# A gated recurrence block on one core: raw weights as single 2 KB blocks in one ring of six, sums written over them, and one order of products for single and twin pairs

## The chip, the cores and the metric

One core of a Trainium2 chip runs the whole program. The metric is the device time of one execution in microseconds, the median of several runs. A profile is one execution taken by the hardware profiler; its span runs from the first to the last instruction.

## The reference, cut to what matters

One decoder layer on 1024 tokens of width 1024, all in float32:

```
proj = x @ w_in -> q | f | i | og | pool_v | gate_a | gate_b        # w_in: 1024 x 7168
a = HGRN2(q, f, i) -> per-head RMSNorm * sigmoid(og) -> @ w_a       # 8 heads, a recurrence over the tokens
b = per-group linear(causal_mean(pool_v) - pool_v) * pool_scale     # 4 groups, w_pool
mix = (sigmoid(gate_a) * a + sigmoid(gate_b) * b) @ w_out
x = LN(alpha * x + mix)
x = LN(alpha * x + relu(x @ w_up)^2 @ w_down)                       # w_up: 1024 x 4096
```

## The kernel before, in words

**Products.** TensorE (PE) multiplies in a rounded float32 form. To keep accuracy each operand is split in a high and a low part: ScalarE (ACT) writes the rounded copy (L118 for weights, a CAST), VectorE (DVE) the rest (L119), and a product takes three matmuls for each 128 rows of depth: high by high, high by low, low by high (L201, L203, L204 in `prod`). A product of `prod` has a depth of 512, so twelve matmuls, and fills one PSUM bank of 128 x 512.

**Pairs.** Large products are done by Strassen's scheme in Winograd's form: a weight of 1024 rows and 2 x 128 columns is four blocks b11, b12, b21, b22 of 512 x 128 (2 KB in each partition), the tokens four parts a11 to a22 with sums s1 to s4, and seven products take the place of eight. `pair` (L263) holds this for one such pair of column blocks. Its operands are t0 = b11, b21, t3 = b22 - b12, t2 = t3 + b11, t4 = b21 - t2, t1 = b12 - b11 and b22; its products are p1 (t0), p2 (b21), p7 (t3), p6 (t2), p5 (t1), p4 (t4) and p3 (b22). p1, p6, p5 and p3 add up in one PSUM bank, `ps["a"]`; p7 and p4 in `ps["z"]`; p2 has `ps["c"]`. Between them results are taken out: after p1 and p6 ACT copies bank a (L271), after p7 it copies bank z, after p5 DVE adds bank a onto the copy of z (L275). Each of these must end before the next product adds onto that bank.

**Who uses pairs.** In the head stage, one at a time through `run`: `head_inputs` (eight, L643), `output_gates` (four, L674), `pooled` (four, L732) and `gates` (eight, L688). Then `a_pair` (four, L1001) on w_a, two together in `run`, so that their products alternate. Then the up projection on w_up: pairs 0 and 1 together, pair 2 threaded between them (`run_second`, L373), and pairs 3 to 15 singly (L1211). A flag `twin` chooses between two orders: pairs that run together do p1, p2, p7, p4, p6, p5, p3, one operand at a time; single pairs do p1, p2, then t3 and t2 together with p6, p7, then t1 and t4 together with p5, p4, then p3 (L346).

**Raw weights.** Weights come from HBM over the SP queue into raw tiles. `raw_tile` (L206) is a ring of two tiles of 4 KB in each partition; one holds two blocks (b11 and b12, or b21 and b22). Two neighbouring blocks come in one load of 512 KB (L217), two that lie apart in two loads of 256 KB (L223). The sums t are written to a ring of two 2 KB tiles (`w_diff`, L239); t2 and t4 are written over the first of them. So b11 and b12 are free when t1 has been formed, b21 and b22 when b22 has been split. In the up projection every second pair uses a ring of its own (`up_raw_tile`, L1144), and every second w_a pair `mg_raw` (L998). Others borrow `raw_tile` too: the block b22 of the values at the start (L445), rows of w_out (L585), and the weights of the pooled linear (`pool_products`, L708). Split operands go to a ring of ten w tiles of 2 KB (L233), two for each operand.

**What sets the order.** The framework plans the order of every queue ahead of time, with a timing model: at each point an engine gets the earliest instruction of the program that the plan has ready, so that products of the next pair fill in where the pair's own products wait. `high_priority` moves an instruction up; all matmuls of a product but its first have it, so that a product that has begun goes through. The order is then fixed; on the chip each engine's queue, SP's too, runs in that order, and an instruction that waits holds up those behind it. Tiles are given out in the same plan when an earlier one is released.

**The end of the heads.** After the last head's recurrence (`hgrn`, L806; its matmuls L875, L898, L915, L918) the program has gates 4, the pooled linear of group 0, gates 5, group 1, gates 6, groups 2 and 3 and gates 7 (L942). `pool_products` loads pooled rows (L719, by way of L594), splits them in w tiles (L118) and multiplies (L105 to L107). The gates store their sigmoids from L699.

The order of a pair's steps, as it is returned:

```
        return (
            ((t0,), ((t0, p1),)),
            ((b_21,), ((b_21, p2),)),
            *(
                (((t3,), ((t3, p7),)), ((t4,), ((t4, p4),)), ((t2,), ((t2, p6),)), ((t1,), ((t1, p5),)))
                if twin
                else (((t3, t2), ((t2, p6), (t3, p7))), ((t1, t4), ((t1, p5), (t4, p4))))
            ),
            ((b_22,), ((b_22, p3),)),
        )
```

Of the kernel before, what the change touches and what calls it, by code (L numbers as in the profile page):

```python
# [16 lines left out]
P = 128  # L17
# [26 lines left out]
def tile_hybrid_block(  # L44
# [161 lines left out]
    def raw_tile():  # L206
        return wq.tile([P, CH, 2, P], F32, tag="raw", name=nm("raw"), bufs=2)

    def w_blocks(src, c1, c2, tile_of=raw_tile):

        raw = tile_of(), tile_of()

        def load(*which):
            for kh in range(2):
                rows_of = src[kh * HALF : (kh + 1) * HALF, :].rearrange("(k p) c -> p k c", p=P)
                if c2 == c1 + P and len(which) == 2:
                    done = nc.sync.dma_start(  # L217
                        out=raw[kh].rearrange("p k n c -> p k (n c)"), in_=rows_of[:, :, c1 : c1 + 2 * P]
                    )
                else:  # L220
                    for n in which:
                        c = (c1, c2)[n]
                        done = nc.sync.dma_start(out=raw[kh][:, :, n], in_=rows_of[:, :, c : c + P])  # L223
            return done

        return raw, load

    def loaded_blocks(*args):
        raw, load = w_blocks(*args)
        load(0, 1)  # L230
        return raw
# [31 lines left out]
    def pair(raw, rooms, takes, pz_tag="pj", twin=False, pc_tag="pj"):  # L263


        b11, b12, b21, b22 = raw if len(raw) == 4 else (raw[kh][:, :, n] for kh in range(2) for n in range(2))
# [76 lines left out]
        def b_22():  # L343
            return w_part(b22)

        return (  # L346
            ((t0,), ((t0, p1),)),
            ((b_21,), ((b_21, p2),)),
            *(
                (((t3,), ((t3, p7),)), ((t4,), ((t4, p4),)), ((t2,), ((t2, p6),)), ((t1,), ((t1, p5),)))  # L350
                if twin
                else (((t3, t2), ((t2, p6), (t3, p7))), ((t1, t4), ((t1, p5), (t4, p4))))
            ),
            ((b_22,), ((b_22, p3),)),
# [47 lines left out]
    with tc.tile_pool(name="xr", bufs=8, side="right", reuse_waits="tile") as xr:  # L402
# [42 lines left out]
        def raw_tile_rows():  # L445
            return [raw_tile().rearrange("p k n c -> p (k n c)").rearrange("p (k c) -> p k c", c=HALF) for _ in range(2)]
# [171 lines left out]
    with tc.tile_pool(name="tmp", bufs=1, side="right", reuse_waits="tile") as tmp:  # L618
# [89 lines left out]
        def pool_products(g):  # L708
# [6 lines left out]
            raw = raw_tile().rearrange("p k n c -> p (k n c)")[:, : 2 * 2 * P].rearrange("p (k c) -> p k c", c=2 * P)  # L715
# [229 lines left out]
        nxt = head_inputs(0, (None, None, "p6", None, None))  # L945
# [55 lines left out]
        def a_pair(p):  # L1001
            raw = loaded_blocks(w_a, 2 * p * P, (2 * p + 1) * P, raw_tile if p % 2 else mg_raw)
            room = mg_tile("room", 4)
            takes = [gated(2 * p + i, u, p < 2) for u in range(2) for i in range(2)]
            return pair(raw, (c_tile, room, room), takes, "hg", True)
# [76 lines left out]
    with tc.tile_pool(name="wo", bufs=1, side="right", reuse_waits="tile") as mp:  # L1082
        st1 = [None] * 8
        g1, b1 = ln_params(lambda: f(act_tile()).rearrange("p a b -> p (a b)"), ln1_g, ln1_b)
        for k2 in range(0, KT, 2):
            raw = raw_rows(w_out, k2, 1)
            for k in range(2):
                n = len(wo)
                out_row(raw[:, k], (
# [46 lines left out]
    with tc.tile_pool(name="up", bufs=1, side="right", reuse_waits="tile") as up:  # L1136
# [15 lines left out]
        def units(i, raw):  # L1152
# [28 lines left out]
            return pair(raw, (c_tile,) * 3, (take(0), last, take(2), take(3)), "hg", i < 2, "tr" if i == 2 else "pj")  # L1181
# [4 lines left out]
        blocks = [up_blocks(i) for i in range(2)]  # L1186
        for _, load in blocks:
            load(0, 1)
        pairs = [units(i, raw) for i, (raw, _) in enumerate(blocks)]
# [212 lines left out]
```

## Time and profile before

| | |
|---|---|
| median of 3 runs | 1461.98 us (1461.56 to 1463.47) |
| the profiled execution | 1460.19 us, span 1458.5 us |
| mean granted TensorE clock | 0.996 |
| loads of w_in, 256 KB each | 64, median 3.4 us from issue to landing |
| loads of w_up, 512 KB each | 30, median 4.2 us |
| a split of 128 x 512 | 620 ns on ACT (L118), 702 ns on DVE (L119) |
| taking a bank out | 582 ns on ACT (L271), 681 ns on DVE (L275) |

How to read the profile: busy times are the sum of an engine's instructions, in us and as a share of the span; PE is TensorE's matmuls and PEld its weight loads, which overlap them. A matmul's shown time includes its way through the array: matmuls of one stream start every 0.23 us though each is shown with 0.39 us, so a product's time is read from start to start. A row of the timeline has the start, the duration, the engine, the line, the operation and the tiles as out<-in; brackets at its end give the idle time of that engine just before and what ended it. A row of waits has the waiting instruction, what it waited for, and total us, times and the longest. A landing time runs from the issue of a load to its last byte.

### The profile page before, as it was taken

To read this page: it belongs to the slowest core of one execution; us is meant where nothing else is said; L and a number is where in the kernel's file an instruction comes from. 1 tells how busy PE (TensorE), PEld (TensorE's weight loads), DVE (VectorE), ACT (ScalarE), POOL (GpSimd) and SP (SyncE) were. 2 spreads that over 40 slices of the span, in tenths; PEclk is the share of its full clock that TensorE was granted. 3 is DMA by queue.
4 is the path that set the end of the run, shared out by engine and by line. 5 is a ranking of instruction groups with operands and counts; after the bars stand their busy time and mean duration, and the time that the engine had idled before them with its cause. 6 is when DMAs were issued, how large, how long until landed. Compare 5 with 4: busy or idle time off the path is not lost.

```text
span 1458.5 us, 20662 instructions
## 1 busy us (share of the span) xinstructions
PE 1436.4 (98%) x7377; PEld 1187.9 (81%) x7377; DVE 1141.6 (78%) x1838; ACT 758.3 (52%) x1383; POOL 58.6 (4%) x244
## 2 busy tenths in 40 slices
PE   8999999999999998999999999999999999999997
PEld 7888888888888886788888878888888888888886
DVE  5967989899898885768985597666666787777977
ACT  5445565666656655556542376555555443333535
POOL 0001001001000010000002100000000100000000
PEclk9999999999999999999999999999999999999999
DMA  7232233323234447897672225444474874445322
GB/s 253 70 126 87 85 98 101 109 75 114 90 99 138 152 132 249 301 299 241 223 247 99 73 94 195 159 146 144 152 261 149 275 260 150 153 141 163 130 73 116
DMA packets 160615, 226.82 MB, mean 156 GB/s; under 512 B 11232, under 2 KB 84480, under 8 KB 160512
## 3 DMA queue, kind: packets, MB, share of 16 engines
q1 hardware_dynamic: 158576, 218.93, 44.7%
q0 software_dynamic: 1152, 4.19, 0.8%
q10 hardware_dynamic: 784, 2.38, 0.5%
q8 instruction: 58, 0.95, 0.3%
q14 instruction: 45, 0.37, 0.1%
HBM read 154.16 MB, written 71.30 MB: 155 GB/s over the span
## 4 chain that ended last, share of the span: by engine, by line
PE 94%; DVE 3%; DMA 1%; ACT 1%; issue 0%; SPq 0%; DVEq 0%
PE ps_pj L201 16%; PE ps_pj L203 16%; PE ps_pj L204 16%; PE ps_pj L1283 4%; PE ps_pj L1285 4%; PE ps_pj L1284 4%; PE ps_pj L106 3%; PE ps_pj L107 3%; PE ps_pj L105 2%; PE ps_tr L1285 1%; PE ps_tr L1283 1%; PE ps_tr L1284 1%; PE ps_sc L201 1%; PE ps_sc L203 1%; PE ps_sc L204 1%; PE ps_hg L203 1%
## 5 line engine op out<-in xcount | busy, mean ns | idle before, releaser
L201 PE MATMUL ps_pj<-act,w 128*128 128x512 f32 x1068 | 421.6, 395 | 0.4 <-ACT act L123 0.2
L203 PE MATMUL ps_pj<-act,w 128*128 128x512 f32 x1068 | 415.1, 390 | 0.5 <-DVE act L124 0.5
L204 PE MATMUL ps_pj<-act,w 128*128 128x512 f32 x1068 | 414.1, 390 | 0.0
L201 PEld LDWEIGHTS ps_pj<-act,w 128*128 128x128 f32 x1068 | 200.6, 188 | 42.8 <-ACT act L123 0.6
L204 PEld LDWEIGHTS ps_pj<-act,w 128*128 128x128 f32 x1068 | 200.5, 188 | 42.3
L203 PEld LDWEIGHTS ps_pj<-act,w 128*128 128x128 f32 x1068 | 200.6, 188 | 40.6 <-DVE act L124 0.9
L118 ACT CAST w<-t 128x512 fp32r<-128x512 f32 x170 | 104.7, 620 | 105.0 <-PE ps_pj L203 53.8
L118 ACT CAST w<-raw 128x512 fp32r<-128x512 f32 x143 | 88.2, 620 | 117.3 <-PE ps_pj L203 62.5
L119 DVE TENSOR_TENSOR w<-raw,w 128x512 fp32r<-128x512 f32 x143 | 99.8, 702 | 55.2 <-ACT w L118 53.9
L119 DVE TENSOR_TENSOR w<-t,w 128x512 fp32r<-128x512 f32 x170 | 115.9, 685 | 29.6 <-ACT w L118 29.4
L1245 ACT CAST act<-act 128x1024 fp32r<-128x1024 f32 x66 | 66.9, 1050 | 107.9 <-issue 35.0
L1246 DVE TENSOR_TENSOR act<-act,act 128x1024 fp32r<-128x1024 f32 x66 | 79.3, 1220 | 18.5 <-ACT act L1245 15.8
L1285 PE MATMUL ps_pj<-act,act 128*128 128x512 f32 x240 | 92.9, 389 | 0.0
L1284 PE MATMUL ps_pj<-act,act 128*128 128x512 f32 x240 | 92.9, 389 | 0.0
L1283 PE MATMUL ps_pj<-act,act 128*128 128x512 f32 x240 | 92.4, 389 | 0.0
L275 DVE TENSOR_TENSOR c<-c,ps_pj 128x512 f32<-128x512 f32 x95 | 64.5, 681 | 18.0 <-PE ps_pj L204 13.4
L271 ACT COPY c<-ps_pj 128x512 f32<-128x512 f32 x96 | 55.2, 582 | 12.8 <-PE ps_pj L204 12.8
L817 DVE RECIPROCAL tC<-tA 128x128 f32<-128x128 f32 x64 | 54.1, 904 | 0.0
L1284 PEld LDWEIGHTS ps_pj<-act,act 128*128 128x128 f32 x240 | 45.1, 188 | 9.4
L1285 PEld LDWEIGHTS ps_pj<-act,act 128*128 128x128 f32 x240 | 45.1, 188 | 9.4
L1283 PEld LDWEIGHTS ps_pj<-act,act 128*128 128x128 f32 x240 | 45.1, 188 | 9.3
L241 DVE TENSOR_TENSOR t<-raw,raw 128x512 f32<-128x512 f32 x43 | 29.6, 689 | 21.9 <-DMA raw<-in_w_in_dram 19.7
(415 smaller groups left out, 2719.8 us busy)
## 6 DMA issues: line engine op xcount, KB each, us to landing
h<-c SPq DMA_DIRECT2D x106, 256.0 KB, 2.1
act<-h SPq DMA_DIRECT2D x78, 256.0 KB, 2.9
raw<-in_w_in_dram SPq DMA_DIRECT2D x64, 256.0 KB, 3.4
draw<-in_w_down_dram SPq DMA_DIRECT2D x16, 1024.0 KB, 7.8
raw<-in_w_up_dram SPq DMA_DIRECT2D x30, 512.0 KB, 4.2
raw<-in_w_in_dram SPq DMA_DIRECT2D x18, 512.0 KB, 4.0
hf<-h SPq DMA_DIRECT2D x34, 256.0 KB, 2.9
c<-o SPq DMA_DIRECT2D x24, 256.0 KB, 3.4
```

The lines of the kernel that those rows point to most:

```text
L118: A.copy(hi, src)
L119: V.tensor_sub(lo, src, f(hi))
L201: PE.matmul(ps, wh[:, k], th, start=first and k == 0, stop=False, skip_group_check=True)
L203: PE.matmul(ps, wh[:, k], tl, start=False, stop=False, skip_group_check=True)
L204: PE.matmul(ps, wl[:, k], th, start=False, stop=k == CH - 1, skip_group_check=True)
L271: A.copy(t, ps)
L275: V.tensor_add(t, t, ps)
L1245: A.copy(hi, src)
L1246: V.tensor_sub(lo, src, f(hi))
L1283: PE.matmul(ps, hh[:, w], wh, start=fresh and n == 0, stop=False, skip_group_check=True)
L1284: PE.matmul(ps, hh[:, w], wl, start=False, stop=False, skip_group_check=True)
L1285: PE.matmul(ps, hl[:, w], wh, start=False, stop=n == M - 1, skip_group_check=True)
```

## The change

One ring of six 2 KB tiles, `block_tile`, takes the place of both `raw_tile` and the ring of sums. A single pair's four blocks have a tile each and a load of 256 KB each, in the order b11, b21, b12, b22, with a fifth tile for t asked for ahead of b22. In t4 the difference b12 - b11 is written over b12 (t1 then only splits it), t becomes b22 - (b12 - b11), and b21 - t is written over b21. The flag `twin` is gone: every pair has the order that twin pairs had, and the sum of c21 is taken after p6. In the up projection all pairs but pair 1 use the ring (pair 1 keeps up's own tiles); `up_raw_tile`'s second turn for odd pairs is gone, and the loads of w_down start behind the load of b22 of the last pair but one. The wide loads stay for w_a pairs 0 and 2. The values' b22, the rows of w_out and the pool weights use the ring's tiles, the first two with a load for each tile.

```diff
-    def raw_tile():
-        return wq.tile([P, CH, 2, P], F32, tag="raw", name=nm("raw"), bufs=2)
...
+    def block_tile(shape=(CH, P)):
+        return wq.tile([P, *shape], F32, tag="raw", name=nm("raw"), bufs=6)
+
+    def wide_block(src, kh, c, t):
+
+        rows_of = src[kh * HALF : (kh + 1) * HALF, :].rearrange("(k p) c -> p k c", p=P)
+        done = nc.sync.dma_start(out=t, in_=rows_of[:, :, c : c + t.shape[2]])
+        return t, done
...
+    def loaded_blocks(src, c1, c2, done=None):
+
+        raw = {}
+        for i in ((0, 0), (1, 0), (0, 1), "t", (1, 1)):
+            raw[i] = block_tile(), None
+            if i != "t":
+                raw[i] = wide_block(src, i[0], (c1, c2)[i[1]], raw[i][0])
+        if done is not None:
+            done.append(raw[1, 1][1])
+        return [raw[i][0] for i in ((0, 0), (0, 1), (1, 0), (1, 1), "t")]
...
-    def w_diff(a, b):
-        t = wq.tile([P, CH, P], F32, tag="t", name=nm("t"), bufs=2)
-        V.tensor_sub(t, a, b)
-        return t
...
         def t3():
-            c["t"] = w_diff(b22, b12)
+            c["t"] = block_tile() if t is None else t
+            V.tensor_sub(c["t"], b22, b12)
             return w_part(c["t"])
 
-        def t2():
-            if not twin:
-                V.tensor_add(c["t"], c["t"], b11)
-            return w_part(c["t"])
-
         def t4():
-            if not twin:
-                V.tensor_sub(c["t"], b21, c["t"])
-                return w_part(c["t"])
-            V.tensor_add(c["t"], c["t"], b11)
+            V.tensor_sub(b12, b12, b11)
+            V.tensor_sub(c["t"], b22, b12)
             V.tensor_sub(b21, b21, c["t"])
             return w_part(b21)
 
+        def t2():
+            return w_part(c["t"])
+
         def t1():
-            return w_part(w_diff(b12, b11))
+            return w_part(b12)
...
                 c[21] = copied(rooms[1], ps["a"])
-                if twin:
-                    takes[2](added(c[21], ps["z"]))
+                takes[2](added(c[21], ps["z"]))
 
         def p4(w):
             prod(ps["z"], w, "a22", False)
-            if not twin:
-                with tc.high_priority(PRIO):
-                    takes[2](added(c[21], ps["z"]))
...
+        return tuple(
+            ((operand,), ((operand, product),))
+            for operand, product in ((t0, p1), (b_21, p2), (t3, p7), (t4, p4), (t2, p6), (t1, p5), (b_22, p3))
         )
...
-        raw = raw_tile().rearrange("p k n c -> p (k n c)").rearrange("p (k c) -> p k c", c=HALF)
-        rows_of = src[k2 * P : (k2 + 2) * P, cc * HALF : (cc + 1) * HALF].rearrange("(k p) c -> p k c", p=P)
-        nc.sync.dma_start(out=raw, in_=rows_of)
+        raw = [block_tile((HALF,)) for _ in range(2)]
+        for k in range(2):
+            nc.sync.dma_start(out=raw[k], in_=src[(k2 + k) * P : (k2 + k + 1) * P, cc * HALF : (cc + 1) * HALF])
         return raw
...
-            raw = raw_tile().rearrange("p k n c -> p (k n c)")[:, : 2 * 2 * P].rearrange("p (k c) -> p k c", c=2 * P)
+            raw = block_tile((2, 2 * P))
...
-        def up_blocks(i):
-            return w_blocks(w_up, i * 2 * P, i * 2 * P + P, up_raw_tile if i % 2 else raw_tile)
...
         for i in range(3, NP):
-            raw, load = up_blocks(i)
-            w_load = load(0, 1)
+            done = []
+            raw = loaded_blocks(w_up, i * 2 * P, i * 2 * P + P, done)
             if i == NP - 2:
                 for part in down_rows(0, ws0):
-                    part(w_load)
+                    part(done[0])
             run(units(i, raw))
```

More of the change, by code (lines that the diff above doesn't have):

```diff
@@ L204, in prod, with wide_blocks @@
                 PE.matmul(ps, wl[:, k], th, start=False, stop=k == CH - 1, skip_group_check=True)
-    def raw_tile():
-        return wq.tile([P, CH, 2, P], F32, tag="raw", name=nm("raw"), bufs=2)
[L209 to L231, printed above, removed]
+    def block_tile(shape=(CH, P)):
[4 more added lines that the diff above has]
+        return t, done
+    def wide_blocks(src, c1, tile_of):
+        raw = [wide_block(src, kh, c1, tile_of().rearrange("p k n c -> p k (n c)"))[0] for kh in range(2)]
+        return [raw[kh][:, :, n * P : (n + 1) * P] for kh in range(2) for n in range(2)]
+    def loaded_blocks(src, c1, c2, done=None):
[7 more added lines that the diff above has]
+        return [raw[i][0] for i in ((0, 0), (0, 1), (1, 0), (1, 1), "t")]
     def w_tile():
@@ L261, in c_late, with pair @@
         return c_tile(False)
-    def pair(raw, rooms, takes, pz_tag="pj", twin=False, pc_tag="pj"):
-        b11, b12, b21, b22 = raw if len(raw) == 4 else (raw[kh][:, :, n] for kh in range(2) for n in range(2))
+    def pair(raw, rooms, takes, pz_tag="pj", pc_tag="pj"):
+        b11, b12, b21, b22, t = raw if len(raw) == 5 else (*raw, None)
         c, ps = {}, {}
@@ L445, in raw_tile_rows @@
         def raw_tile_rows():
-            return [raw_tile().rearrange("p k n c -> p (k n c)").rearrange("p (k c) -> p k c", c=HALF) for _ in range(2)]
+            return [block_tile((1, HALF)) for _ in range(4)]
         def load_block(tiles, kh, nh, ks=None):
@@ L1001, in a_pair @@
         def a_pair(p):
-            raw = loaded_blocks(w_a, 2 * p * P, (2 * p + 1) * P, raw_tile if p % 2 else mg_raw)
+            cols = 2 * p * P, (2 * p + 1) * P
+            raw = loaded_blocks(w_a, *cols) if p % 2 else wide_blocks(w_a, cols[0], mg_raw)
             room = mg_tile("room", 4)
             takes = [gated(2 * p + i, u, p < 2) for u in range(2) for i in range(2)]
-            return pair(raw, (c_tile, room, room), takes, "hg", True)
+            return pair(raw, (c_tile, room, room), takes, "hg")
         def unpark(*which):
@@ L1088, in tile_hybrid_block @@
                 n = len(wo)
-                out_row(raw[:, k], (
+                out_row(raw[k], (
                     (lambda: (row_tile(), row_tile())) if n < 10 else
@@ L1179, in last @@
                 put(6, s4)
-            return pair(raw, (c_tile,) * 3, (take(0), last, take(2), take(3)), "hg", i < 2, "tr" if i == 2 else "pj")
-        def up_blocks(i):
-            return w_blocks(w_up, i * 2 * P, i * 2 * P + P, up_raw_tile if i % 2 else raw_tile)
[L1186 to L1189, printed above, removed]
+            return pair(raw, (c_tile,) * 3, (take(0), last, take(2), take(3)), "hg", "tr" if i == 2 else "pj")
+        blocks = loaded_blocks(w_up, 0, P), wide_blocks(w_up, 2 * P, up_raw_tile)
+        pairs = [units(i, raw) for i, raw in enumerate(blocks)]
         run(pairs[0][1:2])
```

11 lines of the change are left out of this document (1 added, 10 removed).

## The prediction

> **What bounds the kernel now.** I read the page first: the engines' shares, then the chain that ended last.
>
> ```profile
> span 1458.5 us, 20662 instructions
> PE 1436.4 (98%) x7377; PEld 1187.9 (81%) x7377; DVE 1141.6 (78%) x1838; ACT 758.3 (52%) x1383; POOL 58.6 (4%) x244
> PE 94%; DVE 3%; DMA 1%; ACT 1%; issue 0%; SPq 0%; DVEq 0%
> ```
>
> PE is busy for 1436.4 of 1458.5 us and carries 94% of the chain. The change alters no matmul, so all that it can win is 22.1 us of idle PE. The view of stages says where that idle time lies (columns: stretch, its length, busy us of each engine, granted clock, DMA share, GB/s).
>
> ```profile
> 0.00:30.00 30.00, 26.09 (x137) 22.18 (x137) 13.89 (x29) 16.71 (x31) 2.07 (x28) 1.00 0.79 281
> 30.00:574.90 544.90, 543.86 (x3400) 451.05 (x3400) 469.71 (x889) 315.45 (x680) 37.29 (x202) 1.00 0.35 112
> 574.90:592.00 17.10, 10.35 (x42) 7.54 (x41) 9.22 (x16) 7.69 (x21) 0.00 (x0) 0.80 0.77 255
> 592.00:858.00 266.00, 265.85 (x1203) 219.62 (x1201) 202.32 (x330) 123.56 (x215) 14.78 (x6) 1.00 0.61 205
> 858.00:870.00 12.00, 10.80 (x45) 8.02 (x44) 12.00 (x22) 7.82 (x15) 0.00 (x0) 1.00 0.30 89
> 870.00:1136.00 266.00, 266.00 (x1175) 220.29 (x1174) 178.12 (x271) 157.17 (x266) 0.00 (x0) 1.00 0.50 171
> 1450.00:1458.50 8.50, 0.00 (x0) 0.00 (x0) 5.34 (x9) 0.29 (x1) 0.00 (x0) 0.63 0.32 123
> ```
>
> The first 30 us (3.9 us idle, waiting for x and starting up) and the last norm (8.5 us) are out of the change's reach. The heads (30 to 574.9) lose 1.0 us, the up projection (870 to 1136) nothing. One place is worth something: 574.9 to 592, where PE idles 17.10 - 10.35 = 6.75 us; 858 to 870 adds 1.20 us. The view of PE's waits names them:
>
> ```profile
> PE ps_pj L105 <- ACT w L118: 4.7, 1, 4.7
> PE ps_hg L915 <- DVE st L883: 1.2, 1, 1.2
> PE ps_pj L106 <- DVE w L119: 0.8, 1, 0.8
> ```
>
> At 577 us the last head's recurrence is still running and the next matmul in PE's queue is the pooled product of group 0 (L105). The timeline shows why that one is late, and what else could have run:
>
> ```profile
> 559.09 0.93 SPq L223 DMA_DIRECT2D raw<-in_w_in_dram  x2
> 561.72 1.89 SPq L223 DMA_DIRECT2D raw<-in_w_in_dram  x2
> 564.90 0.34 SPq L594 DMA_DIRECT2D v<-po  x1
> 573.10 0.34 SPq L699 DMA_DIRECT2D gb<-c  x1
> ```
> ```profile
> 582.18 0.62 ACT L118 CAST w<-og 128x512 fp32r<-128x512 f32 x1 [2.75 <-DMA og<-po]
> 582.85 0.79 PE L105 MATMUL ps_pj<-w,q 128*128 128x512 f32 x1 [4.66 <-ACT w L118]
> ```
> ```profile
> 587.41 1.13 ACT L118 CAST w<-raw 128x512 fp32r<-128x512 f32 x2
> ```
> ```profile
> raw<-in_w_in_dram SPq DMA_DIRECT2D x4, 256.0 KB, 5.9
> ```
>
> SP stands still from 564.90 to 573.10 on a store (gb<-c), so the pooled rows (og<-po) come late. gates(5), whose products need nothing from that head, got its four blocks at 559.09 and 561.72, each landing about 5.9 us later, as it waited for the two 4 KB tiles that gates(4) and the pool weights of group 0 held. Its first casts stand at 587.41, behind the pooled rows. PE ran out of other products.
>
> **The change part by part.** One product is twelve matmuls:
>
> ```profile
> 899.76 0.39 PE L201 MATMUL ps_sc<-act,w 128*128 128x512 f32 x1
> 902.25 0.39 PE L204 MATMUL ps_sc<-act,w 128*128 128x512 f32 x1
> 902.48 0.39 PE L201 MATMUL ps_pj<-act,w 128*128 128x512 f32 x1
> 902.98 0.58 ACT L271 COPY c<-ps_sc 128x512 f32<-128x512 f32 x1
> 910.41 0.39 PE L204 MATMUL ps_sc<-act,w 128*128 128x512 f32 x1
> 910.64 0.39 PE L201 MATMUL ps_pj<-act,w 128*128 128x512 f32 x1
> 910.89 0.69 DVE L275 TENSOR_TENSOR c<-c,ps_sc 128x512 f32<-128x512 f32 x1 [1.65 <-PE ps_sc L204]
> ```
>
> 902.48 - 899.76 = 2.72 us a product, 19.0 us a pair.
>
> *Sums in place.* A single pair had four sums on DVE (L241 twice, L284, L289) and has four after it (one in t3, three in t4), of the same shape; the seven splits stay. Nothing gained or lost in DVE work. They are bunched: the operand of p4 now has three sums in a row ahead of its split, 3 x 0.69 = 2.1 us. Operands are made up to five ahead (ten w tiles, two each), so 2.1 us against 4 x 2.72 = 10.9 us of products costs nothing; without that lead it would cost up to 1.4 us a pair.
>
> *The ring.* Six tiles of 2 KB replace two of 4 KB and two of 2 KB: 12 KB before and after. A pair takes five (four blocks and the sum). The sixth lets the next pair's b11 load a whole pair ahead; b21 follows when b11 of the pair before is read for the last time (t4), b12 after the split of t4, b22 after that of t1. Before, the next pair's four blocks waited for t1 and for the split of b22, the very last operand. So in the heads the blocks come earlier by up to three operands, about 8 us. There PE doesn't wait for them, so that wins nothing, except before 592: gates(5) has b11 and b21 some 8 us earlier, about 551 instead of 559 to 562, landed by 557. Then p1 and p2 of gates(5), 2 x 2.72 = 5.4 us, can be put ahead of the pooled products. Bounds: nothing (the planner keeps the pooled rows first) and all 6.75 us. I take 5.4, the two products whose blocks come early; what is late next is the rest of the 6.75, the recurrence's own L915.
>
> *The up projection* had two tile pairs in turn (raw and up's own), a whole pair of lead; now the ring alone. b22 of the next pair is asked for after t1, two products' operands from the end, and is needed three operands into the next pair: about 5 x 2.72 - 2 = 11 us against a landing of 3.4 us (256 KB row below), so it is covered. If SP's queue held it for 8 us, as at 564.90, each pair could lose a few us. The w_down loads are now issued behind the fourth block of the last pair but one:
>
> ```profile
> 1075.66 1.99 SPq L1132 DMA_DIRECT2D draw<-in_w_down_dram  x4
> ```
> ```profile
> 1136.40 0.39 PE L1283 MATMUL ps_pj<-act,act 128*128 128x512 f32 x1
> ```
>
> That is later by about a pair, 19 us, at 1095; 4 MB at the 255 to 281 GB/s of the two busiest stages above is 15 to 16 us more, so they are there at 1111, some 25 us ahead of first use. Nothing.
>
> *More and smaller loads.*
>
> ```profile
> raw<-in_w_in_dram SPq DMA_DIRECT2D x64, 256.0 KB, 3.4
> raw<-in_w_up_dram SPq DMA_DIRECT2D x30, 512.0 KB, 4.2
> raw<-in_w_in_dram SPq DMA_DIRECT2D x18, 512.0 KB, 4.0
> ```
>
> 18 loads of w_in become 36 and 30 of w_up become 58; w_a and w_out add 8: 54 issues more, at 0.3 to 0.5 us each on a queue that is mostly waiting. Two halves of 3.4 us overlap each other, so a full 512 KB lands later than 4.2 us and no later than 6.8; the first half sooner. Hidden by PE's backlog; uncovered it is 2.6 us a pair. The Trainium skill speaks against this part: "DMA: Bandwidth & Descriptors", Bandwidth, tells authors to batch loads to 1 MiB or more. By that rule alone the sum would move toward that 2.6 us for each pair; the rows agree that the bytes cost more in halves, and say that PE isn't waiting for them.
>
> At the start b22 of the values takes four tiles, so two are free and head 0's first two blocks load some 45 us early. Their operands would take four of ten w tiles in a stage that uses eight. Bounds: -1.0 us (the idle time of that stage filled) to about +3 (a split of 0.62 + 0.69 us late at two steps); I take 0.
>
> *The order of products.* p6, p7, p5, p4, p3 becomes p7, p4, p6, p5, p3. The data dependences are the same: p6, p5 and p3 add onto one bank and each waits for the evacuation of the last, as p4 does for p7's copy. Before, another product of the pair stood between each. Now p6, p5, p3 are neighbours and PE needs a foreign product in between. The copy ended 902.98 + 0.58 - 902.25 = 1.31 us after the product's last matmul began, the add 1.17 us after; laid bare, less the 0.23 us until the next matmul's slot, each is about 1.0 us. The order is planned by readiness: p6 can go ahead of p4, p4 between p6 and p5, and p1 or p2 of the next pair between p5 and p3. One such product covers 2.72 us. In the heads DVE is 469.71/544.90 = 86% busy and the add after p5 comes later:
>
> ```profile
> 201.22 0.39 PE L204 MATMUL ps_pj<-act,w 128*128 128x512 f32 x1
> ```
> ```profile
> 203.91 0.67 DVE L275 TENSOR_TENSOR f<-f,ps_pj 128x512 f32<-128x512 f32 x1
> ```
>
> Here it ended 3.36 us after the last matmul began, 3.13 us after its slot: 0.4 us more than one product covers; two cover it. Bounds: 0, and 38 single pairs x 3 x 1.0 = 114 us. I take 1.0 us in all, near the lower end, because the row of the heads shows PE full with the same dependences.
>
> The Trainium skill, "Perfetto Trace Analysis", Matmuls, says that independent matmul groups should rotate through PSUM banks so that one's evacuation overlaps the next. The new order of a single pair goes against it; the old one agreed, with its idle-free stages. By the rule the sum is the rival "bare evacuations" below.
>
> **Sum.** The profiled execution took 1460.19 us (span 1458.5). -5.4 + 1.0 = -4.4 gives 1455.8. The median of the runs, 1461.98, lies 1.8 above it, so the forecast is **1457.6 us**.
>
> **Rivals.** (1) *The gap stays.* The pooled products hold their place ahead of gates(5), because SP's stall and the recurrence set that order and not the weights. For it: og<-po is what ended ACT's wait at 582.18. Then -0 + 1.0: 1463.0, between 1460 and 1464.5.
>
> (2) *Bare evacuations: slower.* If in the heads only one foreign product is ready between p5 and p3, each of the 24 pairs there pays 0.4 us, 10 us, and the gap stays: 1472. It decides from the point where p2 of the next pair has no operand when p5 ends. Against it: earlier blocks make operands earlier. For it: four pj banks, which two running pairs fill. If nothing is ready at even one of the three places, 38 x 1.0 = 38 us: 1500.
>
> (3) *Late blocks.* SP's queue holds b21 or b22 in the up projection; 12 pairs x 1 us, gap closed: 1469. Against it: the 11 us above.
>
> (4) *It doesn't do what it says*: the planner keeps the old product order wherever readiness decides; then only the ring counts, 1456.6, inside the forecast.
>
> **How the numbers follow.** Forecast with (4) 0.47, gap stays 0.23, bare evacuations 0.24 (of it 0.04 for the large form), late blocks 0.06. The forecast's own range is 1454 (all 6.75 and the 1.2 us won: 1461.98 - 7.95) to 1459. The range over the cases is 1454 to 1474: it holds (1), the small form of (2) and (3), and leaves the large form out. Two kernels can be told apart from about 0.2%, 2.9 us: below 1459.1 is faster, 0.47; up to 1464.9 the same, 0.23; slower 0.30.
>
> **What would show it.** In the changed profile: between 575 and 592 PE's idle time falls from 6.75 to about 1 to 2 us and L118 casts of gates(5) stand ahead of those of the pooled rows; from 30 to 575 and from 870 to 1136 PE's busy time stays within 1 us of the stretch; no wait of L201 on L271 or L275 exceeds 1 us in total; loads of w_up land around 3.4 us. Bare evacuations would show as waits of L201 for L271 or L275, tens of times; late blocks as waits of L118 for raw that pass on to PE. I am wrong if PE's idle time grows in the heads or in the up projection, or if a gap opens elsewhere because the new order moves other work.

## The result and the profile after

The changed kernel takes **1467.94 us** (median of 9 runs, 1464.55 to 1471.46), the kernel before 1462.68 us beside it (9 runs). The ratio is **1.0032** (95% interval 1.0019 to 1.0045): slower by 4.7 us where 4.4 us of gain were forecast. The nine runs spread over 7 us and the granted clock of a run goes with them: 0.999 in the fastest, 0.993 in the slowest. The profiled execution took 1467.26 us, its span is 1465.5 us.

The head of the page, and the view of stages (stretch, its length, busy us of each engine with the number of its instructions, granted clock, DMA share, GB/s):

```profile
span 1465.5 us, 20835 instructions
PE 1441.2 (98%) x7377; PEld 1189.9 (81%) x7377; DVE 1137.4 (78%) x1838; ACT 756.8 (52%) x1383; POOL 56.2 (4%) x244
```
```profile
0.00:30.00 30.00, 25.60 (x127) 22.12 (x128) 13.09 (x28) 17.31 (x31) 2.06 (x28) 1.00 0.86 298
30.00:574.90 544.90, 540.17 (x3375) 446.60 (x3374) 468.68 (x888) 312.03 (x677) 35.34 (x202) 1.00 0.35 111
574.90:592.00 17.10, 17.10 (x83) 14.42 (x82) 9.21 (x18) 8.71 (x21) 0.00 (x0) 0.93 0.64 207
592.00:858.00 266.00, 261.66 (x1170) 214.57 (x1169) 195.43 (x323) 119.71 (x211) 14.39 (x6) 0.99 0.62 207
858.00:870.00 12.00, 11.29 (x52) 8.47 (x51) 11.71 (x21) 7.45 (x14) 0.00 (x0) 1.00 0.18 56
870.00:1136.00 266.00, 265.14 (x1170) 219.13 (x1169) 175.83 (x270) 154.78 (x263) 0.00 (x0) 1.00 0.50 167
```

Read the matmul counts, not only the busy time: both kernels have the same 7377 matmuls, so the number begun by a given time says how far each has come, and it also sees matmuls that run slowly, which count as busy. The gap at 574.9 to 592 is gone: 83 matmuls and no idle time, where 42 had 6.75 us of it. But the kernel got there late: 10 matmuls fewer in the first 30 us, 25 fewer from 30 to 574.9. By 592 it is only 3 ahead (3581 against 3578, counted in one stretch from 0; the rows count a matmul that lies across a border twice). From 592 to 858 it begins 33 fewer than before (1170 against 1203), with 4.34 us idle against 0.15. By 870 it is 23 behind (4799 against 4822), at 0.23 us each 5.3 of the 7.0 us by which the two profiled spans differ: most of the loss is made before the up projection starts. From 870 to 1136 it loses 5 more.

The view of PE's waits (waiting instruction, what for, us in total, times, longest) names new entries that the kernel before doesn't have:

```profile
PE ps_pj L201 <- ACT c L264: 3.2, 2, 2.1
PE ps_pj L105 <- ACT q L118: 3.0, 1, 3.0
PE ps_pj L457 <- ACT act L123: 2.0, 1, 2.0
PE ps_hg L204 <- DVE w L119: 0.9, 1, 0.9
```

The third stands at the start. The timeline of ACT there, of before and then of after:

```profile
7.56 0.58 ACT L123 CAST act<-ps_tr 128x512 fp32r<-128x512 f32 x1
10.59 0.62 ACT L118 CAST w<-b 128x512 fp32r<-128x512 f32 x1 [2.45 <-DMA b<-in_w_in_dram]
```
```profile
7.51 0.62 ACT L118 CAST w<-b 128x512 fp32r<-128x512 f32 x1 [2.48 <-DMA b<-in_w_in_dram]
10.55 1.14 ACT L118 CAST w<-b 128x512 fp32r<-128x512 f32 x2 [2.42 <-DMA b<-in_w_in_dram]
11.71 1.05 ACT L123 CAST act<-ps_tr 128x512 fp32r<-128x512 f32 x2
```

Before, ACT made the first activation part (L123) at 7.56 and then waited for the third row of the values' weights. After, the casts of the third and fourth row stand ahead of it in ACT's queue, so it comes at 11.71. PE, whose first real product needs it, pauses (before, then after):

```profile
10.13 0.48 PE L477 MATMUL ps_pj<-w,act 128*128 128x512 f32 x1
```
```profile
12.32 0.50 PE L457 MATMUL ps_pj<-w,act 128*128 128x512 f32 x1 [2.01 <-ACT act L123]
```

The edit didn't touch this code's order. The plan drew a new order around the new ring.

### The profile page after: what moved, and what is told of

Its sections match the earlier page's. It is cut to its first block, busy times and chain, and to the rows that moved or that the text cites. A ratio compares the mean times of both kernels' runs of the same rounds, so it can differ in the third digit from the quotient of the medians.

```text
span 1465.5 us, 20835 instructions
## 1 busy us (share of the span) xinstructions
PE 1441.2 (98%) x7377; PEld 1189.9 (81%) x7377; DVE 1137.4 (78%) x1838; ACT 756.8 (52%) x1383; POOL 56.2 (4%) x244
## 4 chain that ended last, share of the span: by engine, by line
PE 85%; DMA 7%; DVE 5%; issue 1%; ACT 1%; SPq 1%; DVEq 0%; ACTq 0%
PE ps_pj L201 15%; PE ps_pj L203 15%; PE ps_pj L204 15%; PE ps_pj L1260 4%; PE ps_pj L1261 4%; PE ps_pj L1259 4%; DMA raw<-in_w_in_dram 2%; PE ps_pj L105 2%; PE ps_pj L107 2%; PE ps_pj L106 2%; PE ps_tr L1261 1%; PE ps_tr L1260 1%; PE ps_tr L1259 1%; PE ps_hg L204 1%; DMA draw<-in_w_down_dram 1%
## 5 line engine op out<-in xcount | busy, mean ns | idle before, releaser
L201 PE MATMUL ps_pj<-act,w 128*128 128x512 f32 x1068 | 422.9, 397 | 5.2 <-ACT c L264 3.2
L204 PE MATMUL ps_pj<-act,w 128*128 128x512 f32 x1068 | 414.3, 391 | 0.0
L118 ACT CAST w<-raw 128x512 fp32r<-128x512 f32 x311 | 191.7, 622 | 251.1 <-PE ps_pj L203 157.6
L119 DVE TENSOR_TENSOR w<-raw,w 128x512 fp32r<-128x512 f32 x311 | 211.6, 686 | 79.6 <-ACT w L118 76.7
L201 PEld LDWEIGHTS ps_pj<-act,w 128*128 128x128 f32 x1068 | 200.9, 188 | 50.4 <-ACT c L264 3.8
L204 PEld LDWEIGHTS ps_pj<-act,w 128*128 128x128 f32 x1068 | 200.8, 188 | 42.4
L264 ACT COPY c<-ps_pj 128x512 f32<-128x512 f32 x96 | 55.7, 582 | 11.7 <-PE ps_pj L204 6.2
L273 DVE TENSOR_TENSOR raw<-raw,raw 128x512 f32<-128x512 f32 x43 | 29.6, 689 | 26.0 <-DMA raw<-in_w_in_dram 22.5
L1130 ACT ACTIVATE c<-c 128x512 f32<-128x512 f32 x61 | 38.7, 634 | 1.5
L1129 ACT ACTIVATE c<-c 128x512 f32<-128x512 f32 x46 | 29.1, 633 | 15.5 <-DVE c L268 15.5
```

Of the source, the lines that this page charges most:

```text
L118: A.copy(hi, src)
L119: V.tensor_sub(lo, src, f(hi))
L201: PE.matmul(ps, wh[:, k], th, start=first and k == 0, stop=False, skip_group_check=True)
L204: PE.matmul(ps, wl[:, k], th, start=False, stop=k == CH - 1, skip_group_check=True)
L264: A.copy(t, ps)
```

## The experiments

All ratios are to the kernel before on the same chip, with a 95% interval; 0.001 is 1.5 us. "The ring" stands for the ring of six with the sums in place, "the order" for single pairs in the twin pairs' sequence.

**1. The two parts alone.** My first theory (A) was that the ring wins and the order loses.

```diff
 # ring alone: after, with the flag and the old sequence of single pairs back
+    def pair(raw, rooms, takes, pz_tag="pj", twin=False, pc_tag="pj"):
 # order alone: before, every pair as a twin
-    def pair(raw, rooms, takes, pz_tag="pj", twin=False, pc_tag="pj"):
+    def pair(raw, rooms, takes, pz_tag="pj", twin=True, pc_tag="pj"):
```

> The ring of six with the sums in place, but single pairs in their old order (t3 and t2 with p6, p7, then t1 and t4 with p5, p4). Theory A (the ring wins, the order loses): the idle time of PE at 575 to 592 is closed by 5.4 us as in the changed kernel, the waits of L201 on copies of a bank (3.2 us in the changed kernel) are gone, and the time is 4 to 6 us below before, 1457 to 1459. Rival B (any change re-plans all queues, and the kernel before had a lucky plan): PE's idle time falls in one place and opens in another, and the time lies within 3 us of before or above it. Rival C (the ring is what costs): it is slower than before by 4 us or more.

> The kernel before, with its two rings, and every single pair in the twin pairs' order of operands and products. Theory A: the gap at 575 to 592 stays (some 6 us of idle PE) and bare evacuations come on top, 3 to 6 us: 1466 to 1469. Rival B: within 3 us of the changed kernel either way, with gaps at places that neither had. Rival C: as fast as before, 1461 to 1464.

Measured: the ring alone 1.0054 (1.0042 to 1.0066), the order alone 1.0008 (1.0000 to 1.0017). It is the other way round, and theory A falls: the part that I gave a gain costs most, the part that I feared costs 1.2 us. The two don't add up: together they stand at 1.0032, so with the ring in place the order takes 3.2 us off, and neither figure is a price that holds in the other kernel. The ring alone has the start's wait too (2.0 us), the order alone doesn't.

**2. Two other orders of the changed kernel.** The third group's pooled products ahead of gates 6, and p6 ahead of p4 in single pairs of the heads.

```diff
-("gates", 6), ("pool_products", 2), ("pool_products", 3), ("gates", 7),
+("pool_products", 2), ("gates", 6), ("pool_products", 3), ("gates", 7),
```
```diff
+            steps[3:5] = [((t4, t2), ((t2, p6), (t4, p4)))]
```

> The changed kernel, with the pooled linear of group 2 put ahead of gates 6, so that group 3's weights don't ask for a room that group 2's store has only just left. If the new gap at 642 to 645 us (3.0 us of idle PE, and matmuls at a lower clock behind it, 5.5 us in that stretch of 50 us) comes from that wait of ACT on the store, it goes and the time falls by 3 to 5 us below the changed kernel, to 1463 to 1465. If another wait stands behind it, the time stays within 1.5 us of the changed kernel's 1467.9.

> The changed kernel, with p6 ahead of p4 in single pairs (operands t4 and t2 made together, then p6, then p4, and the sum of c21 after p4), so that a product of the pair itself stands between p7 and p4 and between p6 and p5. Theory A (bare evacuations cost 3 to 5 us): the waits of L201 on a bank's copy fall from 3.2 us to under 1 us, and the time falls by 2 to 4 us to 1464 to 1466. Rival B: those waits go or stay, but the time is set by other gaps of the new plan and lies anywhere from 1460 to 1472.

Measured: 1.0085 (1.0070 to 1.0099) and 1.0064 (1.0052 to 1.0076). Both are slower than the changed kernel. With p6 ahead of p4 PE waits for casts instead (2.9 us, L201 on L118) and for the recurrence; with pooled products put earlier three evacuations are bare (4.8 us, L201 on L264). Neither order is a cure.

**3. Is it the recurrence?** The last step of the last head's recurrence on DVE (before, then after):

```profile
589.58 0.74 DVE L932 SCALAR_TENSOR_TENSOR og<-ps_tr,prm,og 128x512 f32<-128x512 f32 x1
```
```profile
598.22 0.75 DVE L912 SCALAR_TENSOR_TENSOR og<-ps_tr,prm,og 128x512 f32<-128x512 f32 x1
```

It ends 8.6 us later. Theory B: earlier blocks let the pairs' operand work go ahead of the recurrence on DVE (86% busy in the heads), and PE lacks work in the end. Four runs: the recurrence put first in the plan of after and, as control, of before; a ring of five with a tile of its own for t; and the start's order taken back.

```diff
-                with tc.high_priority(PRIO_LAST) if (h, u) == (HEADS - 1, 1) else nullcontext():
+                with tc.high_priority(PRIO_LAST if (h, u) == (HEADS - 1, 1) else 300):
```
```diff
 # ring of five
-        return wq.tile([P, *shape], F32, tag="raw", name=nm("raw"), bufs=6)
+        return wq.tile([P, *shape], F32, tag="raw", name=nm("raw"), bufs=5)
...
-            c["t"] = block_tile() if t is None else t
+            c["t"] = wq.tile([P, CH, P], F32, tag="t", name=nm("t"), bufs=1) if t is None else t
```
```diff
 # start as before
-        w = parts(b11)
+        w = parts(b11[:2])
+        with tc.issue_after(made_hi["a11", "first"]):
+            w += parts(b11[2:])
```

The last one comes close to the old order and isn't quite it: all four first casts of the activations stand ahead of the third row now, where before only one did.

> The changed kernel with one edit: the instructions of the heads' recurrence take precedence in the order that the plan writes out, so that fewer of VectorE's instructions for the pairs stand ahead of each half's last step (550 ahead of the seventh head's second half where the changed kernel has 560, 358 ahead of the fourth head's first where it has 375). Theory B (the ring lets the pairs' operand work go ahead of the recurrence on VectorE, the recurrence ends later, and TensorE lacks work at the end of the heads): the last half ends near 590 us where it ended at 598, and the time falls by 3 to 6 us, to 1462 to 1465. Rival R (the loss is made of unrelated places where the plan put the queues in another order: the start's 2 us, the pool weights' 3 us, the 2 us of evacuations): within 1.5 us of the changed kernel, 1466.5 to 1469.5, even though the recurrence ends earlier. A third way, that products then lack operands in the heads because their work stands behind the recurrence: idle time of TensorE from 30 to 550 us grows by over 3 us.

> The kernel before with the same single edit as the run above, as its control: the recurrence takes precedence in the plan. Theory B: there the recurrence was hardly held up, since the pairs' blocks came late (562 instructions ahead of the seventh head's first half's successor, 562 with the edit too), so the time stays within 2 us of the kernel before, 1460 to 1464; what the edit wins in the changed kernel it doesn't win here. Rival R: any new order of the plan costs some us wherever it falls: 1465 or more. If it wins 3 us or more here too, then the recurrence was late before as well, and the edit tells nothing about the ring.

> The changed kernel with a ring of five 2 KB tiles and one 2 KB tile by itself for the sums, so that the sixth tile no longer carries the next pair's first block a whole pair ahead. Theory B: less lead, so the recurrence is held up less in the fifth to seventh heads' first halves (371 and 402 instructions ahead where the changed kernel has 375 and 417), though hardly less at the last half (562 for 560 and 570 for 583): 1463 to 1466. Rival R: no relation to the lead: 1466.5 to 1470, or worse where the blocks now come late.

> The changed kernel with only the start's order on ScalarE as it was before: the third and fourth casts of the values' rows of blocks stand behind the first casts of the activations, not ahead of them. Both theories take the wait of TensorE at 10.3 to 12.3 us (2.0 us for an act tile) for a cost of that order: the wait goes, and the time falls by 1.5 to 2.5 us, to 1465.5 to 1466.5. If the time stays within 0.7 us, the 2 us are given back later, where TensorE waits for the heads' recurrence and not for its own backlog of products.

Measured: recurrence first 1.0019 (1.0010 to 1.0028), its control 0.9992 (0.9983 to 1.0001), ring of five 1.0013 (1.0000 to 1.0026), **start as before 1.0002 (0.9992 to 1.0012)**. With the recurrence first it did end earlier, at 592.21:

```profile
592.21 0.74 DVE L912 SCALAR_TENSOR_TENSOR og<-ps_tr,prm,og 128x512 f32<-128x512 f32 x1
```

6 us earlier bought about 1.9 us, less than B asked. The start's order, which I put at 1.5 to 2.5 us, took back 4.4, and the kernel stands level with the one before. PE begins early again, and its stages follow:

```profile
10.18 0.48 PE L458 MATMUL ps_pj<-w,act 128*128 128x512 f32 x1
```

```profile
0.00:592.00 592.00, 585.18 (x3596) 485.49 (x3597) 494.08 (x937) 338.84 (x733) 37.97 (x230) 1.00 0.39 125
592.00:870.00 278.00, 273.49 (x1227) 223.04 (x1225) 208.91 (x345) 130.28 (x229) 14.38 (x6) 1.00 0.59 198
```

against these of the kernel before:

```profile
0.00:592.00 592.00, 580.30 (x3578) 480.77 (x3578) 492.82 (x933) 339.85 (x732) 39.36 (x230) 0.99 0.38 125
592.00:870.00 278.00, 276.65 (x1246) 227.65 (x1245) 214.32 (x350) 131.38 (x229) 14.78 (x6) 1.00 0.59 200
```

By 592 it is 18 matmuls ahead, 4.1 us: the filled gap. By 870 it is one behind: 4.51 us idle from 592 to 870, where it was 1.35. What the gap gave is given back there.

**4. The start alone, and the gains together.** The start's new order put into the kernel before; the start taken back in the ring alone; and together with the ring of five and with the recurrence first.

```diff
 # before, with the start's order of after
+            with tc.issue_after(last_hi[0]) if name == "a11" and not kp else nullcontext():
+                in_parts(name, kp, ps)
```

(`last_hi[0]` is the cast of the values' fourth row.)

> The kernel before with one edit: ScalarE's order at the start is that of the changed kernel (the casts of the third and fourth row of the values' first block stand ahead of the first cast of the activations); the rest of VectorE's order in the heads is the same count for count. Theory S (the start's order alone makes most of the loss): TensorE waits some 2 us for an act tile at about 10 us and the time rises by 2 to 4.4 us (4.4 is what taking this order back won in the changed kernel: ratios 1.0032 and 1.0002): 1465.5 to 1468 against 1463.5 for the kernel before. Rival: in the kernel before the 2 us are given back in the 9 us at 575 to 600 us where TensorE waits for the recurrence, and the time rises by less than 1 us.

> The ring alone (single pairs in their old order) with the start's order as it was before. The ring alone stood at a ratio of 1.0054. If the start's order is the ring's only price, taking it back leaves nothing: ratio 0.999 to 1.002. If the ring also holds up the recurrence (theory B: with the ring alone the halves of the sixth to eighth head ended 5 to 18 us later than before, and TensorE idled 22 us from 500 to 700 where it idles 13 before), then 1.002 to 1.005 stay: 1466.5 to 1471.

> The changed kernel with the start's order as before and the ring of five with a tile of its own for the sums. If the two gains add (4.4 us for the start and 2.7 us for the ring of five, from the ratios 1.0032, 1.0002 and 1.0013): ratio 0.9983, 1461, faster than the kernel before. If the second is only the order in which the same idle time is spent at the end of the heads, it doesn't come on top: ratio 0.9995 to 1.001.

> The changed kernel with the start's order as before and precedence for the recurrence. If the gains add (4.4 us and 1.9 us): ratio 0.9989, 1462. If the precedence only moves idle time between 575 to 600 us and 600 to 700 us: ratio 0.9998 to 1.001. TensorE's idle time from 500 to 700 us should stay between 13 and 17 us either way, as in all orders so far but those with the ring alone and with the pooled products put earlier.

Measured: the start in the kernel before 1.0022 (1.0012 to 1.0031), so that order alone costs 3.2 us in a kernel that has nothing else of the change. The ring alone falls from 1.0054 to 1.0011 (0.9997 to 1.0024); ring of five from 1.0013 to 0.9997 (0.9988 to 1.0006); recurrence first from 1.0019 to 1.0018 (1.0009 to 1.0027). With the changed kernel (4.4 us) and the pair of experiment 5 (1.0044 to 1.0033) that makes six pairs that differ by this edit alone: 4.4, 6.3, 2.3, 0.1, 1.6 and 3.2 us, **3.0 on the mean**.

The traces show the price more directly. Read instruction by instruction, the queues of PE, ACT and DVE differ within a pair up to 92 us at most; behind that, three pairs (those of the changed kernel, of the kernel before and of experiment 5) have the same order to the end, and the others differ in a few instructions from 575 us on. So the first 100 us hold this price and little else. The changed kernel, then the one with the start as before:

```profile
0.00:100.00 100.00, 94.82 (x444) 78.63 (x445) 71.93 (x123) 48.49 (x84) 2.79 (x34) 1.00 0.47 159
```
```profile
0.00:100.00 100.00, 96.65 (x456) 80.64 (x457) 72.10 (x123) 50.11 (x87) 2.78 (x34) 1.00 0.49 164
```

That is 12 matmuls, 2.8 us; in the other five pairs it is 14 to 19, 3.2 to 4.4 us, always the same way. It is more than the wait of 1.9 to 2.0 us partly because of the granted clock: in six of the eight profiled kernels with this order it falls behind the wait, in none of the ten without. The first 30 us of the kernel before with this order (0.94, where the kernel before has 1.00):

```profile
0.00:30.00 30.00, 24.73 (x120) 20.93 (x121) 11.81 (x25) 16.43 (x30) 2.06 (x28) 0.94 0.79 281
```

The rest of the scatter arises late, and not only from other orders: in the pair of the changed kernel, with the same queues behind 75 us, PE's wait for the fourth group's pool weights near 640 us is 3.0 us in one and 1.1 in the other.

Theory B falls as the main cause: with the start cured, recurrence first is slower than without (1.0018 against 1.0002).

**5. The gap, filled as predicted.** I had said that earlier blocks would put p1 and p2 of gates(5) ahead of the pooled products. The rows of after (SP, then ACT, then PE):

```profile
546.37 0.38 SPq L212 DMA_DIRECT2D raw<-in_w_in_dram  x1
...
547.58 0.38 SPq L212 DMA_DIRECT2D raw<-in_w_in_dram  x1
```
```profile
586.27 0.62 ACT L118 CAST w<-v 128x512 fp32r<-128x512 f32 x1 [0.17 <-DMA v<-po]
586.80 1.66 ACT L118 CAST w<-raw 128x512 fp32r<-128x512 f32 x3
```
```profile
591.18 0.39 PE L201 MATMUL ps_pj<-act,w 128*128 128x512 f32 x1
```

The blocks are asked for 13 us earlier than before (546.4 against 559.1), more than predicted, and then lie for some 37 us: their first cast still stands behind the pooled rows' and p1 of gates(5) starts at 591.18, before it was 589.50. What filled the gap were products of gates(4), whose operands had been cast by 563 us. So theory Q: the order, not the weights, keeps gates(5) out. One edit puts it ahead, in four kernels:

```diff
-("pool_products", 0), ("gates", 5), ("pool_products", 1),
+("gates", 5), ("pool_products", 0), ("pool_products", 1),
```

> The changed kernel with one edit: gates(5) stands ahead of the first group's pooled products in the program, so that the plan puts p1, p2 and p7 of gates(5) ahead of them in TensorE's queue. Theory Q (the queue's order, not the weights, kept gates(5) out of the gap): its first product starts near 570 instead of 591, the idle time from 500 to 700 us falls from 16.5 to about 11, and the time falls by 4 to 6 us, from a ratio of 1.0032 to about 0.9995 (1462 to 1463.5). Rival: idle time there is bound by the recurrence and the pooled rows behind it, whatever fills it; it moves and stays at 13 to 17 us: ratio 1.0025 to 1.004.

> The same edit, with the start's order as before too. Theory Q: both gains add, ratio 0.996 to 0.998, 1457 to 1460, which is where the prediction had the change. Rival: nothing on top of the start's gain, ratio 0.9995 to 1.001.

> The kernel before, without the ring, with gates(5) ahead of the first pooled products. Its blocks are asked for at 559 to 562 and land about 6 us later, 565 to 568, so p1 and p2 could start at about 569 all the same. If the order alone decides: the gap fills here as well, ratio 0.996 to 0.998, and the ring isn't needed for it. If the earlier blocks are needed as well: p1 comes later, the gap stays at more than half, ratio 0.9985 to 1.001.

> Ring of five with a tile of its own for the sums, the start as before, and gates(5) ahead of the first pooled products. It stood at 0.9997 without the last edit. Theory Q: 0.996 to 0.998. Rival: 0.9990 to 1.0005.

Measured: in the changed kernel 1.0044 (1.0030 to 1.0058), with the start as before 1.0033 (1.0022 to 1.0043), in the kernel before 1.0033 (1.0022 to 1.0045), with ring of five and start 0.9991 (0.9982 to 0.9999). In the first of them p1 of gates(5) starts near 570, as theory Q wanted, 21 us earlier than in the changed kernel:

```profile
570.43 0.39 PE L201 MATMUL ps_pj<-act,w 128*128 128x512 f32 x1
```

The time gets worse all the same, and PE's idle time from 500 to 700 us hardly moves: 7.9 us against 8.1 in the changed kernel (the 16.5 of the expectation isn't what the view shows there). That is the rival's outcome. The stages of the second and the third kernel:

```profile
0.00:592.00 592.00, 584.67 (x3591) 484.93 (x3591) 492.10 (x932) 338.05 (x731) 37.96 (x230) 1.00 0.38 122
592.00:870.00 278.00, 272.37 (x1213) 222.26 (x1214) 210.29 (x343) 128.44 (x226) 14.40 (x6) 0.99 0.60 203
```
```profile
0.00:592.00 592.00, 581.77 (x3590) 483.22 (x3591) 493.32 (x935) 337.69 (x721) 39.43 (x230) 1.00 0.38 123
592.00:870.00 278.00, 269.55 (x1200) 219.16 (x1200) 204.84 (x331) 128.42 (x230) 14.75 (x6) 0.99 0.59 201
```

Both are 12 to 13 matmuls ahead of the kernel before at 592, and 33 and 46 behind it from there to 870. Getting ahead by 592 is no gain by itself, with the ring or without it (where 4.0 of the gap's 6.75 us stay idle). That the work used as filling is then missing behind the gap is my reading; no run shows it apart from the waits that each new order brings. Theory Q is right about the order and wrong about the time. Of these four only the last comes out below the kernel before, 1462.16 us against 1462.87, 0.7 us in the medians and 1.3 by the ratio. It is hardly more than level, and the kernel before with the recurrence first (0.9992) is as fast without the ring.

## Why the prediction was wrong

- **What bounds the kernel** was right: PE, with one gap worth naming. What failed is that I took that gap's idle time for reachable time. The changed kernel has none of it and is slower. Two readings beside it were wrong. I put the first 30 us out of the change's reach: they lost 10 matmuls. And idle time isn't all that can be won or lost: busy time grew by 4.8 us with the same matmuls, since slow ones count as busy (the last section).
- **The ring, -5.4 us: this step failed.** Its first half held and went further than predicted (blocks 13 us earlier, not 8). The second half, that p1 and p2 of gates(5) are put ahead of the pooled products, didn't happen: ACT's queue kept them behind. That was half of the rival "the gap stays": the pooled rows held their place, but the gap was filled by other products. And where an edit did put them ahead, the gain was given back between 592 and 870.
- **The start, taken as 0: mis-sized.** It measured 3.0 us over six pairs, the upper end of my bound (-1 to +3), by another mechanism: I looked at spare w tiles and late splits, and what cost was ACT's order at 10 us. It comes with the ring (both rings have it, the order alone doesn't). With it taken back the change measures 1.0002. So 5.4 us of gain that didn't come and 3.0 us of cost make 8.4 of the 9.1 us between forecast and result (9.8 with the 4.4 us of the changed kernel's own pair); what remains is within the scatter. That 1467.94 lies in the range of 1454 to 1474 is luck: the range reached so far up for bare evacuations and late blocks, and the start's order was in none of the cases. The sign of being wrong that I named did come, PE's idle time in the heads (30 to 574.9) grew from 1.0 to 4.7 us.
- **The order of products, 1.0 us**: 1.2 us alone, the size that I had, but the interval reaches down to nothing and with the ring the sign was the other (experiment 1). In the changed kernel two evacuations were bare for 3.2 us, beyond the 1 us that I had allowed. The longer one shows how, in ACT's timeline and PE's:

```profile
562.25 0.62 ACT L118 CAST w<-raw 128x512 fp32r<-128x512 f32 x1 [1.85 <-PE ps_pj L203]
566.78 0.28 ACT L903 ACTIVATE tH<-ps_hg 128x128 f32<-128x128 f32 x1 [3.90 <-PE ps_hg L898]
...
570.94 1.28 ACT L676 ACT_TABLE_LOAD   x1
572.23 0.60 ACT L676 ACTIVATE c<-ps_pj 128x512 f32<-128x512 f32 x1
572.72 1.07 ACT L264 COPY c<-ps_pj 128x512 f32<-128x512 f32 x2
```
```profile
573.36 0.50 PE L201 MATMUL ps_pj<-act,w 128*128 128x512 f32 x1 [2.06 <-ACT c L264]
```

  The copy of p7 for p4 was planned behind the recurrence's reads; ACT stood idle for 3.9 us waiting for those, then loaded a table (1.28 us) and made a sigmoid, and the copy that PE needed came at 572.72. I had asked whether PE has a foreign product in between, not whether ACT is free. The version with the start as before has these waits as well (2.7 us) and is level, so they don't make the loss by themselves. The Trainium skill, "Perfetto Trace Analysis", Matmuls, asks for independent groups that rotate through the banks; the order that goes against it cost 1.2 us here, so other groups did cover nearly all, as far as that kernel shows.
- **Sums in place, and more and smaller loads: nothing**, right to within 1 us. The up projection, with nearly all loads halved, keeps PE at 265.14 of 266 us; its one wait is 0.9 us for a split of DVE's (L204 on L119), which the ring alone has too and the kernel before hasn't. The loads land sooner than I had them:

```profile
raw<-in_w_in_dram SPq DMA_DIRECT2D x100, 256.0 KB, 3.1
raw<-in_w_up_dram SPq DMA_DIRECT2D x56, 256.0 KB, 3.0
```

  3.0 us against 4.2 for the 512 KB of before. The rule of the Trainium skill, "DMA: Bandwidth & Descriptors", Bandwidth (batch to 1 MiB or more), has no cost to show where PE isn't waiting for loads. "Late blocks" didn't come.
- **It doesn't do what it says** didn't hold either: blocks and products were moved as the diff says.

What stays open: why the plan sets the start's casts in another order when the ring changes, and why time won before 592 is lost again by 870: seven of the kernels here are ahead of the kernel before at 592, and none at 870. Of the latter the traces show single pauses only, another one in each kernel. In the changed kernel it is the fourth group's pool weights, whose cast waits for a tile that a store still holds:

```profile
643.94 0.62 ACT L118 CAST q<-raw 128x512 fp32r<-128x512 f32 x1 [3.95 <-DMA pb<-q]
```

PE waits 3.0 us for it (the second entry of its waits) and goes on slowly behind it, which the last section prices at another 1.6 us: 4.6 of the 7.6 us (33 matmuls) lost from 592 to 858. With the start as before, and the same order of queues there, the wait is 1.1 us and nothing slow follows; no run here took it away alone.

## What to carry to other kernels

Where a planner fixes the order of every queue, an edit to one buffer redraws orders far from it: compare the first 30 us and every other stage by the number of matmuls begun, and price the redrawn order before the intended gain. Idle time in a gap is worth something only if the work that fills it isn't missed later; count the work done by a point well behind the gap. An early load gains nothing while the cast that uses it stands behind others in an in-order queue.

## What the runs showed of the hardware that was not expected

A pause of PE can cost more than its length. After the pause of 2.06 us the matmuls run slowly for a while:

```profile
573.94 0.61 PE L204 MATMUL ps_pj<-act,w 128*128 128x512 f32 x1
574.35 0.63 PE L201 MATMUL ps_pj<-act,w 128*128 128x512 f32 x1
...
576.91 0.60 PE L201 MATMUL ps_pj<-act,w 128*128 128x512 f32 x1
577.34 0.40 PE L203 MATMUL ps_pj<-act,w 128*128 128x512 f32 x1
```

From 573.94 to 577.34 they start 0.41 to 0.43 us apart, not 0.23: eight steps, 1.6 us more, shown as busy time. The view of stages gives the clock that was granted there, and behind the 3.0 us wait for the pool weights, where it is the same:

```profile
573.90:577.30 3.40, 3.40 (x9) 2.63 (x8) 0.00 (x0) 0.28 (x1) 0.00 (x0) 0.51 0.52 181
645.60:649.00 3.40, 3.40 (x9) 2.75 (x9) 3.10 (x6) 1.53 (x3) 0.00 (x0) 0.50 0.96 316
```

So each time the clock was halved for some 3.4 us. The kernel before has such a stretch too, behind its own gap (the clock of 0.80 in its row of 574.9 to 592), so of the 4.8 us by which PE's busy time grew these stretches explain little; where the rest lies stays open. It doesn't follow every pause: at 12.32 the changed kernel went on at full pace, while the kernel before with the start's order had five matmuls of 0.63 us soon after its pause there. What decides it no run here shows.
